# Reordering the loads at the stage boundaries of an eight-core hybrid encoder layer, and dividing the last rows' normalisation between engines

## The chip, the cores and the metric

The program runs on all 8 cores of one Trainium2 chip (two dies, cores 0 to 3 and 4 to 7), one batch entry per core, with no exchange between cores. The metric is device microseconds of the slowest core. An execution can fall into a slow state, in which one die's granted TensorE clock (the share of full speed that the records show for it) is lower: 0.936 on die 1 in the profile of the kernel before. The kernel before takes 3447.7 us (median of 4 executions; the slowest of the four, 3532.0 us, was slow).

## The reference, cut to what matters

One layer of a streaming encoder. One input projection feeds three branches; each is gated, projected to 2048 channels, merged by sigmoid gates, projected once more, added to the input and normalised.

```python
q, k, v, logf, g_fox, b_gate, u, g_conv, mq, g_mem = _project(hp, w_in[l], fox_bf[l])
o_fox = _fox_prompt(q, k, v, logf)                    # 1: forgetting attention, 12 heads
c, tail = _short_conv(u, prev0, conv_w[l], conv_b[l]) # 2: conv, 12 chunks of 128 channels
mk, mv = _mem_kv(mem_prompt, w_mem_kv[l])             #    memory keys/values, between the chunks
o_mem = _mem_attn(mq, mk, mv)                         # 3: memory attention, 20 units
m = g1 * y_fox + g2 * y_conv + g3 * y_mem             # 4: merge stage
h = jnp.einsum('btd,de->bte', m, w_o)                 # 5: output stage, 17 row blocks
return _layernorm(DN_ALPHA * x + h, ln_g, ln_b)
```

Per core there are 2048 prompt rows and 64 sample rows. The kernel runs the five stages in this order.

## The kernel before

A helper records operations in program order for each engine and derives the semaphore waits. Two consequences matter. SP and POOL issue the DMAs, each in its own program order: a DMA whose data is not ready holds up every later DMA of that queue. And a tile placed over an old one waits for all recorded users of the old one.

POOL loads all weights into eight ring slots, when TensorE frees one. SP does nearly everything else: stores, branch tiles `a`, merged tiles `mT`, residual rows `x`, gain `lng` and bias `lnb`.

```python
# conv stage: memory tokens are allocated and loaded only after chunk 1
for c in range(1, 12):
    runall(conv_groups(c, c == 1))
    if c == 1:
        E.settle()
        mem_alloc()            # POOL: memT, mkT, mv
    ...                        # memkv(i): first matmuls on memT follow at once

# memory attention: branch tiles 0 to 3 are loaded in the last of the 20 units
        else:
            for b in range(4):
                load_a(0, b, ABUF[b], d_ab[b])
            E.settle()
...
    load_a(0, 4, ABUF[4], d_ab[4])

# merge stage, last pass (u == 2), last column (j == 15), blocks tb = 0..4
    m, g = ...                                  # ACT: g = sigmoid(bank); DVE: m = bank * g
    mb = g[:, 0:n // 2].bitcast(BF16)           # POOL writes the merged block into g's tile,
    ...                                         # SP stores it: mb_scr[j, :, t0:t0+n] <- mb
    if last and j == 15:
        if tb == 0: mT_load(0, 0); mT_load(1, 0)   # columns 0..14 of 256 merged rows each
        if tb == 1: mT_load(0, 1)                  # column 15
        if tb == 2: mT_load(1, 1)

# output stage
for i in range(2, 9):
    mT_tile(i, XT0 + 8192 * (i - 2))
    mT_load(i, 0)                               # seven loads: six of 1 MB, the last of 0.25 MB
...
load_x32(0)                                     # residual rows, 1 MB, behind all of them
S.add(SP, DMA(lng[:], ...)); S.add(SP, DMA(lnb[:], ...))
load_x32(1)
for tc, (t0, tn) in enumerate(TCH):             # 17 row blocks, 64 matmuls each
    ...                                         # 4 of the 8 PSUM banks per block
    # DVE post: x = alpha * x + bank; bn_stats.  This frees the bank.
    load_x32(tc + 2)
    # ACT normalises, DVE multiplies by lng, POOL adds lnb, SP stores;
    # the last 64 rows in four column pieces through the same three engines
```

`g` has two tiles. So ACT can start on a block only after the mb store of the block before the last has landed.

The softmax here doesn't subtract the row's maximum and nothing guards it: scores larger than these inputs give would overflow.

Of the kernel before, what the change touches and what calls it, by code (L numbers as in the profile page):

```python
# [184 lines left out]
D = 2048  # L185
# [167 lines left out]
def build():  # L353
# [632 lines left out]

    kvq = list(range(16))
    trq = []
    for c in range(1, 12):
        runall(conv_groups(c, c == 1))  # L990
        if c == 1:
            E.settle()
            mem_alloc()
        for g in trq:
            mvtrans(g)
        trq = []
        if c >= 2:
            pass
        n = 2 if c <= 5 else 1
        for _ in range(n):  # L1000
            if kvq:
                i = kvq.pop(0)
                memkv(i)
                if i >= 8 and i % 2 == 1:
                    trq.append((i - 8) // 2)
# [49 lines left out]
    for ui, (h, tb) in enumerate(units):  # L1055
        i = ui % 2
        t0, n = TB[tb]
        parts = [(0, n, 0)] if tb < 4 else [(0, PPART, 0), (PPART, n, 1)]
        pts = []
        for mc in range(2):  # L1060
            sb, rs = BK[3 + mc]
            for (a, b, s) in parts:
                for dc in range(2):
                    E.pe(MM(sb[:, a:b], mem["mkT"][s][:, h * 2 + dc, mc * 128:(mc + 1) * 128], mq[i][0][:, dc, a:b], dc == 0, dc == 1),
                         b - a, [r_mk[s][h * 2 + dc], mq[i][1][dc]], [rs])
            p, rp = mpt.next()
            pts.append((p, rp))
            S.add(ACT, ACTF(p[:, 0:n], sb[:, 0:n], AF.Exp, scale=MSCALE), reads=[rs], writes=[rp])
        if ui + 1 < len(units):
            runall(mproj(units[ui + 1][0], units[ui + 1][1], 1 - i))  # L1070
        else:
            for b in range(4):
                load_a(0, b, ABUF[b], d_ab[b])
            E.settle()
        bl, rbl = BK[7]
        for mc in range(2):
            E.pe(MM(bl[:, 0:n], onesb[:, :], pts[mc][0][:, 0:n], mc == 0, mc == 1), n, [pts[mc][1], r_const], [rbl])
        for dc in range(2):
            ob, ro = BK[5 + dc]
            for (a, b, s) in parts:  # L1080
                for mc in range(2):
                    E.pe(MM(ob[:, a:b], mem["mv"][s][:, mc, h * 2 + dc, :], pts[mc][0][:, a:b], mc == 0, mc == 1),
                         b - a, [r_mv[s][h if s == 0 else mc], pts[mc][1]], [ro])
        l, rrl = mrl.next()
        S.add(ACT, ACTF(l[:, 0:n], bl[:, 0:n], AF.Ln), reads=[rbl], writes=[rrl])
        S.add(ACT, ACTF(l[:, 0:n], l[:, 0:n], AF.Exp, scale=-1.0), reads=[rrl], writes=[rrl])
        def fin(h=h, tb=tb, i=i, n=n, l=l, rrl=rrl):
            for dc in range(2):
                ob, ro = BK[5 + dc]
                o, r = mon.next()  # L1090
                S.add(DVE, TT(o[:, 0:n], ob[:, 0:n], l[:, 0:n], ALU.mult), reads=[ro, rrl], writes=[r])
                a, ra = aom.next()
                S.add(POOL, TT(a[:, 0:n], o[:, 0:n], sgm[i][0][:, dc, 0:n], ALU.mult), reads=[r, sgm[i][1][dc]], writes=[ra])
                S.add(SP, DMA(a_scr[2][tb][:, h * 2 + dc, :], a[:, 0:n]), reads=[ra], writes=[r_as[2][tb]], dmasem=d_ao[id(ra)])
        E.later(1.2, fin)
    E.settle()


    load_a(0, 4, ABUF[4], d_ab[4])
    T0 = Region(SB, ABUF[7] + 10240, SB_HI)  # L1100
    gt = T0.ring("gt", 2, [128, 424], F32)
    mt = T0.ring("mt", 2, [128, 424], F32)
# [30 lines left out]
    def mT_load(i, part):  # L1133
        t, rs, n = mT[i]
        t0 = 256 * i
        j0, j1 = ((0, 15), (15, 16))[part] if i < 2 else (0, 16)
        S.add(SP, DMA(t[:, j0:j1, :], mb_scr[j0:j1, :, t0:t0 + n].rearrange("j p t -> p j t")),
              reads=[r_mb[j][b] for j in range(j0, j1) for b in blks(t0, n)],
              writes=[rs[part]] if i < 2 else rs, dmasem=d_mTs[i])

    for u in range(3):
        last = u == 2
# [10 lines left out]
        for j in range(16):  # L1153
# [8 lines left out]
            for tb in range(5):  # L1162
# [32 lines left out]
                if last and j == 15:  # L1195
                    if tb == 0:
                        mT_load(0, 0)
                        mT_load(1, 0)
                    if tb == 1:
                        mT_load(0, 1)  # L1200
                    if tb == 2:
                        mT_load(1, 1)


    for i in range(2, 9):
        mT_tile(i, XT0 + 8192 * (i - 2))
        mT_load(i, 0)
    L0 = Region(SB, XT0 + 7 * 8192, RG0)
    L1 = Region(SB, ABUF[7] + 10240, TT1)
    X0 = Region(SB, ABUF[2], ABUF[5] + 6784)  # L1210
    NR = 4
    x32 = X0.ring("x32", NR, [128, D], F32)
    d_x32 = {id(r): S.dmasem(f"x32_{i}") for i, (t, r) in enumerate(x32.items)}
    d_yo = {id(r): S.dmasem(f"yo_{i}") for i, (t, r) in enumerate(x32.items)}
    r_ln = [Res("lng"), Res("lnb")]
    lng = L0.tile("lng", [128, D], F32, [r_ln[0]])
    lnb = L1.tile("lnb", [128, D], F32, [r_ln[1]])
    r_stat = [Res(f"stat{i}") for i in range(3)]
    stats = [L0.tile(f"stats{i}", [128, 4, 6], F32, [r_stat[i]]) for i in range(3)]
    mv_ = [L0.tile(f"mv{i}", [128, 4], F32, [r_stat[i]]) for i in range(3)]  # L1220
    xq = {}
    def load_x32(tc):
        if tc >= 17:
            return
        t0, tn = TCH[tc]
        t, r = x32.next()
        xq[tc] = (t, r)
        src = I["xp"][t0:t0 + tn, :] if tc < 16 else I["xs"]
        S.add(SP, DMA(t[0:tn, :], src), writes=[r], dmasem=d_x32[id(r)])
    load_x32(0)  # L1230
    S.add(SP, DMA(lng[:], I["ln_g"].partition_broadcast(128)), writes=[r_ln[0]], dmasem=S.dmasem("lng"))
    S.add(SP, DMA(lnb[:], I["ln_b"].partition_broadcast(128)), writes=[r_ln[1]], dmasem=S.dmasem("lnb"))
    load_x32(1)
    HB = Ring(BK)

    def wo_piece(k):
# [5 lines left out]
    for tc, (t0, tn) in enumerate(TCH):  # L1242
        t, r = xq.pop(tc)
        mt_, rmt, _ = mT[tc // 2]
        o0 = t0 - 256 * (tc // 2)
        hb = [HB.next() for _ in range(4)]
        s = tc % 3
        x = t
        def kmm(db, k):
            w, rw = wo_piece(k)  # L1250
            bk, rb = hb[db]
            E.pe(MM(bk[0:tn, :], mt_[:, k, o0:o0 + tn], w[:, db * 512:(db + 1) * 512], k == 0, k == 15), 512,
                 [rmt[1 if k == 15 else 0], rw], [rb])
        def post(db):
            bk, rb = hb[db]
            c = slice(db * 512, (db + 1) * 512)
            S.add(DVE, STT(x[0:tn, c], x[0:tn, c], DN_ALPHA, bk[0:tn, :], ALU.mult, ALU.add), reads=[rb, r], writes=[r])
            S.add(DVE, lambda e, o_=stats[s][0:tn, db, :], i_=x[0:tn, c]: e.bn_stats(out=o_, in_=i_), reads=[r], writes=[r_stat[s]])
        if tc == 0:
            for k in range(16):  # L1260
                for db in range(4):
                    kmm(db, k)
            for db in range(4):
                post(db)
        else:
            for db in range(4):
                for k in range(16):
                    kmm(db, k)
                post(db)
        load_x32(tc + 2)  # L1270
        m = mv_[s]
        S.add(DVE, lambda e, o_=m[0:tn, 0:2], i_=stats[s][0:tn, :, :].rearrange("p a b -> p (a b)"): e.bn_aggr(out=o_, in_=i_),
              reads=[r_stat[s]], writes=[r_stat[s]])
        S.add(ACT, ACTF(m[0:tn, 2:3], m[0:tn, 1:2], AF.Sqrt, bias=epsb[0:tn, 0:1]), reads=[r_stat[s], r_const], writes=[r_stat[s]])
        S.add(DVE, lambda e, o_=m[0:tn, 2:3]: e.reciprocal(out=o_, in_=o_), reads=[r_stat[s]], writes=[r_stat[s]])
        S.add(DVE, STT(m[0:tn, 3:4], m[0:tn, 0:1], -1.0, m[0:tn, 2:3], ALU.mult, ALU.mult), reads=[r_stat[s]], writes=[r_stat[s]])
        npc = 1 if tc < 16 else 4
        w = D // npc
        rp = [r] if npc == 1 else [Res(f"yp{i}") for i in range(npc)]
        for i in range(npc):  # L1280
            c = slice(i * w, (i + 1) * w)
            S.add(ACT, ACTF(x[0:tn, c], x[0:tn, c], AF.Identity, bias=m[0:tn, 3:4], scale=m[0:tn, 2:3]),
                  reads=[r, r_stat[s]], writes=[rp[i]])
            S.add(DVE, TT(x[0:tn, c], x[0:tn, c], lng[0:tn, c], ALU.mult), reads=[rp[i], r_ln[0]], writes=[rp[i]])
            S.add(POOL, TT(x[0:tn, c], x[0:tn, c], lnb[0:tn, c], ALU.add), reads=[rp[i], r_ln[1]], writes=[rp[i]])
            dst = O["y_p"][t0:t0 + tn, c] if tc < 16 else O["y_s"][:, c]
            S.add(SP, DMA(dst, x[0:tn, c]), reads=[rp[i]], dmasem=d_yo[id(r)])

    import contextlib
    es = contextlib.ExitStack()  # L1290
# [80 lines left out]
```

## Time and profile before

| | |
|---|---|
| fast executions | 3446.3 to 3448.4 us |
| profiled execution | slow: die 0 at clock 0.990, die 1 at 0.936; core 0 (3441.8 us) is read |
| TensorE busy, core 0 | 96% |
| chain that ended last | 90% PE |

The wait list of TensorE on core 0: each line names what PE waited for, the total in us, how often, and the longest. Lines whose longest single wait is under 2 us are left out ("...") where nothing below rests on them.

```profile
PE bank L148 <- DMA memT_134<-memT: 17.4, 1, 17.4
PE bank L148 <- DVE x_147_189 L183: 16.5, 1, 16.5
PE bank L148 <- DMA ring_20_62<-w_in: 13.0, 1, 13.0
PE bank L148 <- DMA ring_23_65<-w_in: 10.6, 1, 10.6
...
PE bank L148 <- DMA a_4_112_154<-a_scr_4: 3.6, 1, 3.6
...
PE bank L148 <- DMA a_0_108_150<-a_scr_0: 2.0, 1, 2.0
...
PE bank L148 <- DMA ring_27_69<-w_o: 0.8, 1, 0.8
```

The two w_in lines are the start of the program. The other lines are stage boundaries: 17.4 us at the first memory matmul, 2.0 + 3.6 us at the merge stage, 16.5 us in the output stage.

PE's timeline at the first and third of these gaps. Columns: start us, duration us, engine, source line, operation, output and inputs, and in brackets the idle time ahead of it.

```profile
1123.62 3.02 PE L148 MATMUL bank<-xT_19_61,ring_27_69 128*128 128x420 bf16 x16
1144.05 3.57 PE L148 MATMUL bank<-memT_134,ring_20_62 128*128 128x256 bf16 x16 [17.42 <-DMA memT_134<-memT]
1147.42 2.10 PE L148 MATMUL bank<-memT_134,ring_21_63 128*128 128x256 bf16 x16
...
3214.20 0.58 PE L148 MATMUL bank<-wob_130_172,mT_139_181 128*128 128x512 bf16 x1 [16.46 <-DVE x_147_189 L183]
3214.58 0.63 PE L148 MATMUL bank<-wob_131_173,mT_139_181 128*128 128x512 bf16 x1
3215.01 0.63 PE L148 MATMUL bank<-wob_132_174,mT_139_181 128*128 128x512 bf16 x1
```

The 16 matmuls behind the first gap take 3.57 us, the next 16 of the same shape 2.10. Behind the other gap matmuls soon start 0.43 us apart (3214.58, 3215.01), for about 5 us, and then 0.216. For some us behind such a gap TensorE thus works at half its rate; it is called cold below. A gap therefore costs more than its wait.

SP's own timeline shows why x is late: it stands in SP's queue behind the mT loads.

```profile
3198.91 3.80 SPq L157 DMA_DIRECT2D mT_146_188<-mb_scr  x1
3202.92 4.00 SPq L157 DMA_DIRECT2D x_147_189<-xp  x1
```

The end of the program, after PE's last matmul ends at 3424.4:

```profile
3427.74 2.93 ACT L165 ACTIVATE x_147_189<-x_147_189,mv_157_199 64x512 f32<-64x512 f32 x4 [0.61 <-DVE mv_157_199 L183]
3428.66 4.72 DVE L175 TENSOR_TENSOR x_147_189<-x_147_189,lng_193 64x512 f32<-64x512 f32 x4 [1.01 <-ACT x_147_189 L165]
3429.48 6.24 POOL L175 TENSOR_TENSOR x_147_189<-x_147_189,lnb_194 64x512 f32<-64x512 f32 x4 [6.85 <-DVE x_147_189 L175]
3431.24 5.02 SPq L157 DMA_DIRECT2D y_s<-x_147_189  x4
```

Four pieces follow each other through three engines; POOL is the slowest, 6.24 us for the four.

### The profile page before, as it was taken

The numbers are of one execution on the slowest core, as the hardware profiler recorded it, in microseconds if no ns is written. First come the engines' busy times: TensorE is split into PE (matmuls) and PEld (weight loads), VectorE is DVE, ScalarE is ACT, GpSimd is POOL, SyncE is SP. The second block draws the span as 40 slices with busy tenths as digits, with TensorE's granted clock in tenths as the row PEclk, the third lists the DMA queues.
The fourth block names the chain that finished last, engine by engine and source line by source line (L and its number), as shares of the span: only waits on it lengthen the run. The fifth ranks groups of instructions, "written<-read, shape, count | busy, mean of one in ns | idle before, by whom it ended". The sixth has DMA issues, their size and how long they took to land.

```text
span 3614.3 us, 54781 instructions; the slowest of 8 cores (3434.6 to 3614.3 us)
## 1 busy us (share of the span) xinstructions
PE 3502.0 (97%) x18761; PEld 1845.2 (51%) x18761; DVE 1202.3 (33%) x2092; ACT 1021.2 (28%) x1846; POOL 771.3 (21%) x962
## 2 busy tenths in 40 slices
PE   6999999999999989999999999999999999999898
PEld 3444444544444545555555554555555555555343
DVE  1455555555556722222222221111111111111365
ACT  1455555555555410010104552111111111111111
POOL 1222222222222211111111221000022223332133
PEclk8888888888888999999999999999999999999999
DMA  9423333333222243333323216333455545655743
GB/s 167 97 64 70 70 70 68 66 67 66 66 63 66 46 69 65 68 62 56 61 50 59 47 38 164 90 98 85 116 143 133 138 118 131 141 125 136 206 173 117
DMA packets 183608, 337.45 MB, mean 93 GB/s; under 512 B 31204, under 2 KB 135388, under 8 KB 177000
## 3 DMA queue, kind: packets, MB, share of 16 engines
q0 software_dynamic: 39744, 134.55, 22.9%
q1 hardware_dynamic: 143592, 199.39, 17.9%
q8 instruction: 156, 2.56, 0.3%
q14 instruction: 116, 0.95, 0.1%
HBM read 362.26 MB, written 106.13 MB: 130 GB/s over the span
## 4 chain that ended last, share of the span: by engine, by line
PE 93%; DMA 3%; SPq 1%; ACT 1%; issue 1%; DVE 1%; POOL 1%; POOLq 0%; DVEq 0%; ACTq 0%
PE bank L148 93%; DMA ring_23_65<-w_in 1%; SPq L157 1%; DMA a_scr_3<-ao_59_101 1%; PE bank L154 0%; DMA memT_134<-memT 0%; DMA mb_scr<-gt_114_156 0%; DMA x_147_189<-xp 0%; DMA a_4_112_154<-a_scr_4 0%; ACT rl_83_125 L165 0%; DVE on_85_127 L175 0%; ACT pt_71_113 L165 0%; POOL ao_59_101 L175 0%; DVE acc_78_120 L175 0%; ACT qT_74 L170 0%
## 5 line engine op out<-in xcount | busy, mean ns | idle before, releaser
L175 DVE TENSOR_TENSOR mt_115_157<-bank,gt_113_155 128x424 f32<-128x424 f32 (+1 forms) x120 | 71.8, 598 | 517.8 <-PE bank L148 448.5
L175 DVE TENSOR_TENSOR mt_116_158<-bank,gt_114_156 128x424 f32<-128x424 f32 (+1 forms) x120 | 71.8, 598 | 494.1 <-PE bank L148 463.9
L165 ACT ACTIVATE gt_113_155<-bank,bm_50 128x424 f32<-128x424 f32 (+1 forms) x120 | 73.6, 613 | 506.3 <-PE bank L148 455.6
L165 ACT ACTIVATE gt_114_156<-bank,bm_50 128x424 f32<-128x424 f32 (+1 forms) x120 | 73.6, 613 | 499.4 <-PE bank L148 470.8
L148 PE MATMUL bank<-xT_15_57,ring_20_62 128*128 128x424 bf16 x400 | 84.5, 359 | 17.9 <-DMA ring_20_62<-w_in 13.9
L148 PE MATMUL bank<-qT_70,kT_71 128*128 128x512 bf16 (+4 forms) x246 | 96.2, 391 | 0.0
L148 PE MATMUL bank<-qT_74,kT_75 128*128 128x512 bf16 (+4 forms) x246 | 94.5, 384 | 0.2 <-DVE st_69_111 L183 0.2
L148 PE MATMUL bank<-xT_17_59,ring_26_68 128*128 128x424 bf16 x416 | 86.2, 352 | 4.8 <-ACT qT_74 L170 4.8
L148 PE MATMUL bank<-xT_17_59,ring_22_64 128*128 128x424 bf16 x416 | 86.8, 354 | 4.0 <-ACT qT_70 L170 4.0
L148 PE MATMUL bank<-xT_16_58,ring_24_66 128*128 128x424 bf16 x432 | 90.2, 353 | 0.0
L148 PE MATMUL bank<-xT_19_61,ring_24_66 128*128 128x420 bf16 x432 | 89.4, 351 | 0.0
L148 PE MATMUL bank<-xT_15_57,ring_24_66 128*128 128x424 bf16 x432 | 89.2, 356 | 0.0
L148 PE MATMUL bank<-xT_17_59,ring_24_66 128*128 128x424 bf16 x432 | 88.7, 353 | 0.0
L148 PE MATMUL bank<-xT_18_60,ring_24_66 128*128 128x420 bf16 x432 | 88.2, 351 | 0.0
L148 PE MATMUL bank<-xT_16_58,ring_26_68 128*128 128x424 bf16 x416 | 87.7, 354 | 0.0
L148 PE MATMUL bank<-xT_16_58,ring_22_64 128*128 128x424 bf16 x416 | 87.2, 354 | 0.0
L148 PE MATMUL bank<-xT_15_57,ring_26_68 128*128 128x424 bf16 x416 | 86.6, 354 | 0.0
L148 PE MATMUL bank<-xT_15_57,ring_22_64 128*128 128x424 bf16 x416 | 86.2, 354 | 0.0
L148 PE MATMUL bank<-xT_19_61,ring_22_64 128*128 128x420 bf16 x416 | 84.9, 351 | 0.3
L148 PE MATMUL bank<-xT_18_60,ring_22_64 128*128 128x420 bf16 x416 | 85.1, 351 | 0.0
L148 PE MATMUL bank<-xT_19_61,ring_26_68 128*128 128x420 bf16 x416 | 84.5, 349 | 0.4 <-ACT qT_74 L170 0.2
L148 PE MATMUL bank<-xT_18_60,ring_26_68 128*128 128x420 bf16 x416 | 84.5, 349 | 0.0
(917 smaller groups left out, 7352.2 us busy)
## 6 DMA issues: line engine op xcount, KB each, us to landing
ring_24_66<-w_in POOLq DMA_DIRECT2D x15, 512.0 KB, 6.7
ring_21_63<-w_in POOLq DMA_DIRECT2D x14, 512.0 KB, 8.0
ring_22_64<-w_in POOLq DMA_DIRECT2D x14, 512.0 KB, 7.8
ring_23_65<-w_in POOLq DMA_DIRECT2D x14, 512.0 KB, 6.8
ring_25_67<-w_in POOLq DMA_DIRECT2D x14, 512.0 KB, 8.2
ring_26_68<-w_in POOLq DMA_DIRECT2D x14, 512.0 KB, 6.7
ring_27_69<-w_in POOLq DMA_DIRECT2D x14, 512.0 KB, 6.6
ring_20_62<-w_in POOLq DMA_DIRECT2D x13, 512.0 KB, 7.1
```

What stands on the lines that cost most here:

```text
L148: return lambda e: e.matmul(out, lhsT=lhsT, rhs=rhs, start=start, stop=stop)
L157: return lambda e: e.dma_start(out=out, in_=in_, **kw)
L165: return lambda e: e.activation(out=out, in_=in_, func=func, **kw)
L175: return lambda e: e.tensor_tensor(out=out, in0=in0, in1=in1, op=op)
```

## The change

The intent is to have every load at its place before the stage that needs it begins, and to shorten the end. Cut to its core:

```diff
+    E.later(16.0, mem_alloc)                 # 16 us into conv chunk 1
     for c in range(1, 12):
         runall(conv_groups(c, c == 1))
-        if c == 1:
-            E.settle()
-            mem_alloc()
...
         else:
-            for b in range(4):
+            E.settle()
+        if ui == 8:                          # unit 8 of 20
+            for b in range(5):
                 load_a(0, b, ABUF[b], d_ab[b])
-            E.settle()
...
-    load_a(0, 4, ABUF[4], d_ab[4])
...
                     if tb == 2:
                         mT_load(1, 1)
-    for i in range(2, 9): ... mT_load(i, 0)
-    load_x32(0)
+                        load_x32(0)
+                    if tb == 3:
+                        load_x32(1)
     # after the last column
     ... lng, lnb ...
-    load_x32(1)
+    mT_load(2, 0)
+    load_x32(2)
+    mT_load(3, 0)
...
-        load_x32(tc + 2)
+        load_x32(tc + 3)
+        if tc % 2 == 0 and tc // 2 + 4 < 9:
+            mT_load(tc // 2 + 4, 0)
...
+        # last 64 rows: columns 1536.. on ACT + POOL, the other three pieces on DVE:
+        #   x = (x - mean) * lng;  x = x * rstd + lnb     (two operations of DVE each)
```

The description that came with the change says that the branch tiles are loaded two units ahead. The code loads them in unit 8 of 20, eleven units ahead of the last.

More of the change, by code (lines that the diff above doesn't have):

```diff
@@ L996, in build @@
         trq = []
-        if c >= 2:
-            pass
         n = 2 if c <= 5 else 1
@@ L1139, in mT_load, with x_alloc, load_x32 @@
               writes=[rs[part]] if i < 2 else rs, dmasem=d_mTs[i])
+    L0 = Region(SB, XT0 + 7 * 8192, RG0)
+    L1 = Region(SB, ABUF[7] + 10240, TT1)
+    X0 = Region(SB, ABUF[2], ABUF[5] + 6784)
+    NR = 4
+    xq = {}
+    x32 = None
+    d_x32, d_yo = {}, {}
+    def x_alloc():
+        nonlocal x32
+        x32 = []
+        for i in range(NR):
+            r = Res(f"x32{i}")
+            d_x32[id(r)] = S.dmasem(f"x32_{i}")
+            d_yo[id(r)] = S.dmasem(f"yo_{i}")
+            x32.append([None, r])
+    def load_x32(tc):
+        if tc >= 17:
+            return
+        t0, tn = TCH[tc]
+        e = x32[tc % NR]
+        if e[0] is None:
+            e[0] = X0.tile(f"x32{tc}", [128, D], F32, [e[1]])
+        t, r = e
+        xq[tc] = (t, r)
+        src = I["xp"][t0:t0 + tn, :] if tc < 16 else I["xs"]
+        S.add(SP, DMA(t[0:tn, :], src), writes=[r], dmasem=d_x32[id(r)])
     for u in range(3):
@@ L1200, in build @@
                         mT_load(0, 1)
+                        x_alloc()
                     if tb == 2:
                         mT_load(1, 1)
-    for i in range(2, 9):
-        mT_tile(i, XT0 + 8192 * (i - 2))
-        mT_load(i, 0)
-    L0 = Region(SB, XT0 + 7 * 8192, RG0)
-    L1 = Region(SB, ABUF[7] + 10240, TT1)
-    X0 = Region(SB, ABUF[2], ABUF[5] + 6784)
-    NR = 4
-    x32 = X0.ring("x32", NR, [128, D], F32)
-    d_x32 = {id(r): S.dmasem(f"x32_{i}") for i, (t, r) in enumerate(x32.items)}
-    d_yo = {id(r): S.dmasem(f"yo_{i}") for i, (t, r) in enumerate(x32.items)}
+                        load_x32(0)
+                    if tb == 3:
+                        load_x32(1)
     r_ln = [Res("lng"), Res("lnb")]
@@ L1220, in build @@
     mv_ = [L0.tile(f"mv{i}", [128, 4], F32, [r_stat[i]]) for i in range(3)]
-    xq = {}
-    def load_x32(tc):
-        if tc >= 17:
-            return
-        t0, tn = TCH[tc]
-        t, r = x32.next()
-        xq[tc] = (t, r)
-        src = I["xp"][t0:t0 + tn, :] if tc < 16 else I["xs"]
-        S.add(SP, DMA(t[0:tn, :], src), writes=[r], dmasem=d_x32[id(r)])
-    load_x32(0)
+    for i in range(2, 9):
+        mT_tile(i, XT0 + 8192 * (i - 2))
     S.add(SP, DMA(lng[:], I["ln_g"].partition_broadcast(128)), writes=[r_ln[0]], dmasem=S.dmasem("lng"))
     S.add(SP, DMA(lnb[:], I["ln_b"].partition_broadcast(128)), writes=[r_ln[1]], dmasem=S.dmasem("lnb"))
-    load_x32(1)
+    mT_load(2, 0)
+    load_x32(2)
+    mT_load(3, 0)
     HB = Ring(BK)
@@ L1276, in build @@
         S.add(DVE, STT(m[0:tn, 3:4], m[0:tn, 0:1], -1.0, m[0:tn, 2:3], ALU.mult, ALU.mult), reads=[r_stat[s]], writes=[r_stat[s]])
-        npc = 1 if tc < 16 else 4
-        w = D // npc
-        rp = [r] if npc == 1 else [Res(f"yp{i}") for i in range(npc)]
-        for i in range(npc):
-            c = slice(i * w, (i + 1) * w)
-            S.add(ACT, ACTF(x[0:tn, c], x[0:tn, c], AF.Identity, bias=m[0:tn, 3:4], scale=m[0:tn, 2:3]),
-                  reads=[r, r_stat[s]], writes=[rp[i]])
-            S.add(DVE, TT(x[0:tn, c], x[0:tn, c], lng[0:tn, c], ALU.mult), reads=[rp[i], r_ln[0]], writes=[rp[i]])
-            S.add(POOL, TT(x[0:tn, c], x[0:tn, c], lnb[0:tn, c], ALU.add), reads=[rp[i], r_ln[1]], writes=[rp[i]])
-            dst = O["y_p"][t0:t0 + tn, c] if tc < 16 else O["y_s"][:, c]
-            S.add(SP, DMA(dst, x[0:tn, c]), reads=[rp[i]], dmasem=d_yo[id(r)])
+        dst = O["y_p"][t0:t0 + tn, :] if tc < 16 else O["y_s"]
@@ new lines, in build @@
+        if tc < 16:
+            S.add(ACT, ACTF(x[0:tn, :], x[0:tn, :], AF.Identity, bias=m[0:tn, 3:4], scale=m[0:tn, 2:3]),
+                  reads=[r, r_stat[s]], writes=[r])
+            S.add(DVE, TT(x[0:tn, :], x[0:tn, :], lng[0:tn, :], ALU.mult), reads=[r, r_ln[0]], writes=[r])
+            S.add(POOL, TT(x[0:tn, :], x[0:tn, :], lnb[0:tn, :], ALU.add), reads=[r, r_ln[1]], writes=[r])
+            S.add(SP, DMA(dst, x[0:tn, :]), reads=[r], dmasem=d_yo[id(r)])
+        else:
+            rp = [Res(f"yp{i}") for i in range(4)]
+            for q in rp:
+                q.w = r.w
+                q.r = dict(r.r)
+            c = slice(1536, 2048)
+            S.add(ACT, ACTF(x[0:tn, c], x[0:tn, c], AF.Identity, bias=m[0:tn, 3:4], scale=m[0:tn, 2:3]),
+                  reads=[rp[3], r_stat[s]], writes=[rp[3]])
+            S.add(POOL, TT(x[0:tn, c], x[0:tn, c], lng[0:tn, c], ALU.mult), reads=[rp[3], r_ln[0]], writes=[rp[3]])
+            S.add(POOL, TT(x[0:tn, c], x[0:tn, c], lnb[0:tn, c], ALU.add), reads=[rp[3], r_ln[1]], writes=[rp[3]])
+            for i in range(3):
+                c = slice(i * 512, (i + 1) * 512)
+                S.add(DVE, STT(x[0:tn, c], x[0:tn, c], m[0:tn, 0:1], lng[0:tn, c], ALU.subtract, ALU.mult),
+                      reads=[rp[i], r_stat[s], r_ln[0]], writes=[rp[i]])
+                S.add(DVE, STT(x[0:tn, c], x[0:tn, c], m[0:tn, 2:3], lnb[0:tn, c], ALU.mult, ALU.add),
+                      reads=[rp[i], r_stat[s], r_ln[1]], writes=[rp[i]])
+                S.add(SP, DMA(dst[:, c], x[0:tn, c]), reads=[rp[i]], dmasem=d_yo[id(r)])
+            S.add(SP, DMA(dst[:, 1536:2048], x[0:tn, 1536:2048]), reads=[rp[3]], dmasem=d_yo[id(r)])
```

## The prediction

> All readings are of core 0 (3441.8 us, granted clock 0.989); die 1 was slow (0.936) in the profiled run, so not used. Reference: the two fast timed runs, 3447 and 3448 us.
>
> **What bounds it.** TensorE: 96% busy on the page, 20.0 of 20 us at clock 1.00 in nearly every stretch after 1150 us (windows view), 90% of the chain of waits. Such a change can win only stage-boundary gaps. PE's waits, longest first: memory tokens 17.4 us, residual row 0 (DVE on x, behind its DMA) 16.5, w_in at the start 13.0 and 10.6, branch tiles a_4 3.6 and a_0 2.0.
>
> **Terms (timeline):**
> 1. Memory tokens. Issued at 1130.1, after the settle behind conv chunk 1, landing 13.8 us later; PE stands from 1126.6 to 1144.05. The change issues them 16 us into that chunk (about 1085), where the DMA share is near zero. Wait 17.4 -> 0. PE then runs cold: 16 matmuls take 3.57 us, the next 16 take 2.10. Gain 17.4 + 1.5 = 18.9.
> 2. Branch tiles. Four loads together near the end of the memory stage land after 12.7 to 25 us, the fifth later. Waits 2.0 + 3.6; the groups behind them took 3.99 and 4.36 instead of 2.31, the next 3.63 instead of 3.03. Gain 10. The loads move to memory unit 8. There 6.4 MB hold up the SP queue for an estimated 28 us (rate of the old loads), so an attention store behind them delays POOL and DVE. Rings of 3 and 2 tiles and units of 12.7 us should absorb it; I allow 0 to 3 us.
> 3. Residual rows. Row tile 0 is issued at 3202.9 behind seven mT loads and lands at 3213.3; only then can DVE free the PSUM banks that row 2 needs. Wait 16.5, then about 13 matmuls at 0.427 instead of 0.216 us, 2.7. Issued at about 3170 it lands before row 0 ends (3183.8). Gain 19. POOL's last w_o weight (9.6 us to land, 0.8 us wait) now competes with row tiles: perhaps 1 to 2 us lost.
> 4. Tail. From PE's end (3424.4) to the last y_s issue (3435.9) are 11.5 us, four pieces serially through ACT, DVE and POOL (6.24 us). Now three pieces take two DVE operations each (about 0.7 us) and the fourth ACT plus two on POOL (about 1.5 each), in parallel. Estimate: 2.5 us less.
>
> Sum 50.4, less 1.4 for contention: 49 us. The Trainium skill, "TensorE: Matmul & The Clock Gate", section "What's actually happening", says the default state is throttled and activity releases it; this trace agrees (0.427 -> 0.216 us after the 16.5 us gap).
>
> **Predicted:** 3399 us, 8 in 10 between 3388 and 3417: 1.4% faster. Faster by over 2%: 0.03; within 2%: 0.96; slower by over 2%: 0.01.
>
> **Signs.** PE's wait list has no memT, a_0, a_4 or x over 1 us; memory DMA shows at 1085 to 1110; the three boundaries show clock 1.00; rows run 13.8 us each without a break; the tail after PE is about 15 us instead of 17.4. Failing steps would show as a wait on ring w_o at k = 14, 15 of row 0, on mT, on lng before row 3, or on attention banks around units 10 to 12.
>
> **What would make it wrong.** Row loads ahead of mb stores delaying ACT and the banks; early branch loads stalling attention; denser work lowering the granted clock.

## The result, and the profile after

The changed kernel takes 3406.2 us (median of 4; fast ones 3405.5 to 3406.4) against 3447.7: 41.6 us less (41.1 between the medians of the fast executions). The ratio is 0.988, 95% interval 0.9858 to 0.9903. A ratio is the mean time of one kernel's fast executions over that of the other's from the same rounds, so it is not quite the ratio of the medians. The profiled execution is fast, cores 3395.3 to 3403.9 us.

The wait list of core 0 after, the same view as before:

```profile
PE bank L148 <- DMA ring_20_62<-w_in: 12.7, 1, 12.7
PE bank L148 <- DMA ring_23_65<-w_in: 10.6, 1, 10.6
...
PE bank L148 <- DMA mT_138_180<-mb_scr: 5.2, 1, 5.2
...
PE bank L148 <- DMA ring_27_69<-w_o: 3.4, 1, 3.4
...
PE bank L148 <- DMA ring_26_68<-w_o: 1.4, 1, 1.4
```

memT, a_0, a_4 and x are gone. In their place there are three waits in the output stage: 5.2 us on the first merged tile and 4.8 us (3.4 + 1.4) on the last two w_o weights. PE's timeline shows the mended boundaries and then the new gaps:

```profile
1123.05 3.02 PE L148 MATMUL bank<-xT_19_61,ring_27_69 128*128 128x420 bf16 x16
1125.91 1.91 PE L148 MATMUL bank<-memT_134,ring_20_62 128*128 128x256 bf16 x16
...
1993.11 3.03 PE L148 MATMUL bank<-xT_15_57,ring_20_62 128*128 128x424 bf16 x16
1995.98 2.31 PE L148 MATMUL bank<-a_0_108_150,ring_21_63 128*128 128x424 bf16 x12
...
3136.53 1.59 PE L148 MATMUL bank<-a_4_129_171,ring_27_69 128*128 128x420 bf16 x8
3143.31 1.87 PE L148 MATMUL bank<-wob_130_172,mT_138_180 128*128 128x512 bf16 x4 [5.18 <-DMA mT_138_180<-mb_scr]
...
3158.98 1.02 PE L148 MATMUL bank<-ring_26_68,mT_138_180 128*128 128x512 bf16 x4 [1.42 <-DMA ring_26_68<-w_o]
3163.37 1.86 PE L148 MATMUL bank<-ring_27_69,mT_138_180 128*128 128x512 bf16 x4 [3.37 <-DMA ring_27_69<-w_o]
```

The lines with x4 also show the cold clock again: 1.87 and 1.86 us behind the 5.2 and 3.4 us gaps, 1.02 otherwise.

SP's timeline for the last merge column says where the first gap comes from:

```profile
3131.12 1.91 SPq L157 DMA_DIRECT2D mT_139_181<-mb_scr  x1
3133.08 5.52 SPq L157 DMA_DIRECT2D pv_119_161<-m_scr_3  x1
3138.71 0.37 SPq L157 DMA_DIRECT2D mb_scr<-gt_113_155  x1
3139.12 0.43 SPq L157 DMA_DIRECT2D mT_138_180<-mb_scr  x1
...
3144.82 0.33 SPq L157 DMA_DIRECT2D x_140_182<-xp  x1
3145.72 0.32 SPq L157 DMA_DIRECT2D mb_scr<-gt_113_155  x1
3146.19 1.34 SPq L157 DMA_DIRECT2D x_141_183<-xp  x1
```

Behind mT(0) and mT(1), nearly 1 MB each, SP spends 5.52 us issuing a 210 KB load; the mb store behind it (of block 1) leaves only at 3138.71, after the last merge matmul (end 3138.12). Column 15 of mT(0), which row 0 needs, stands right behind that store: it leaves at 3139.12 and takes 3.8 us to land. That is the first gap on this core. ACT, too, must wait for that store before it may overwrite the gate tile, as its timeline shows:

```profile
3142.85 0.61 ACT L165 ACTIVATE gt_113_155<-bank,bm_50 128x420 f32<-128x420 f32 x1 [11.73 <-DMA mb_scr<-gt_113_155]
```

Behind ACT wait DVE, POOL's merged blocks, and, because POOL issues in order, the last two w_o weights (on cores 2 and 4 it is this late ACT, not mT(0), that ends PE's first wait). POOL's timeline:

```profile
3145.59 1.07 POOL L175 TENSOR_TENSOR gt_114_156<-mt_116_158,pv_117_159 128x420 bf16<-128x420 f32 x1
3146.60 0.57 POOL L157 DMA_DIRECT2D ring_26_68<-w_o  x1
```

Then the weights share the DMA engines with x(0), x(1) and lng. The list of DMA issues (operation, count, KB, us from issue to landing):

```profile
ring_26_68<-w_o POOLq DMA_DIRECT2D x1, 512.0 KB, 12.2
ring_27_69<-w_o POOLq DMA_DIRECT2D x1, 512.0 KB, 16.1
```

The same list of the kernel before:

```profile
ring_26_68<-w_o POOLq DMA_DIRECT2D x1, 512.0 KB, 6.6
ring_27_69<-w_o POOLq DMA_DIRECT2D x1, 512.0 KB, 9.6
```

To see what each stage gained, the rest uses a table made from PE's timeline, all 8 cores averaged: "conv gap" is from the end of conv chunk 1 to the first matmul of chunk 2 (it holds two memory groups, 3.3 us when nothing waits); "merge" is from its first to the end of its last matmul; "output" from there to PE's end; "tail" from PE's end to the end of the span. Conv and memory attention between them take 863.7 to 864.5 us in every run.

| us, mean of cores | conv gap | merge | output | tail | span |
|---|---|---|---|---|---|
| before, fast profile (run base) | 22.5 | 1154.2 | 256.0 | 17.4 | 3439.5 |
| after | 3.3 | 1145.0 | 246.7 | 16.2 | 3400.4 |
| gained | 19.2 | 9.2 | 9.3 | 1.2 | 39.1 |

Each row comes from one execution. How far another one may lie off can be read from a_taildve (below), which is the changed kernel but for the last rows: its output stage is 245.8 us, and the wait at the start of row 0 has a mean of 2.3 us against 3.4.

### The profile page after: what moved, and what is told of

Read it like the earlier page. It is cut to its first block, busy times and chain, and to the rows that moved or that the text cites. A ratio compares the mean times of both kernels' runs of the same rounds, so it can differ in the third digit from the quotient of the medians.

```text
span 3403.9 us, 54778 instructions; the slowest of 8 cores (3395.3 to 3403.9 us)
## 1 busy us (share of the span) xinstructions
PE 3320.0 (98%) x18761; PEld 1788.5 (53%) x18761; DVE 1223.0 (36%) x2094; ACT 1012.8 (30%) x1843; POOL 770.6 (23%) x960
## 4 chain that ended last, share of the span: by engine, by line
PE 94%; DMA 2%; ACT 1%; DVE 1%; POOL 1%; issue 1%; SPq 0%; ACTq 0%; DVEq 0%; POOLq 0%
PE bank L148 94%; DMA ring_23_65<-w_in 1%; DMA ring_27_69<-w_o 0%; PE bank L154 0%; SPq L157 0%; DVE st_69_111 L183 0%; POOL hl_82_124 L175 0%; DVE on_85_127 L175 0%; DVE x_140_182 L183 0%; ACT rl_84_126 L165 0%; ACT qT_74 L170 0%; POOL hl_80_122 L175 0%; ACT qT_70 L170 0%; ACT pt_73_115 L165 0%; POOL hl_81_123 L171 0%
## 5 line engine op out<-in xcount | busy, mean ns | idle before, releaser
L148 PE MATMUL bank<-xT_15_57,ring_20_62 128*128 128x424 bf16 x400 | 81.6, 351 | 16.7 <-DMA ring_20_62<-w_in 12.7
L148 PE MATMUL bank<-xT_17_59,ring_26_68 128*128 128x424 bf16 x416 | 82.7, 342 | 6.0 <-ACT qT_74 L170 6.0
L148 PE MATMUL bank<-xT_17_59,ring_22_64 128*128 128x424 bf16 x416 | 82.8, 342 | 5.0 <-ACT qT_70 L170 5.0
L148 PE MATMUL bank<-xT_16_58,ring_24_66 128*128 128x424 bf16 x432 | 86.1, 342 | 0.0
L148 PE MATMUL bank<-xT_19_61,ring_24_66 128*128 128x420 bf16 x432 | 85.4, 340 | 0.0
L148 PE MATMUL bank<-xT_17_59,ring_24_66 128*128 128x424 bf16 x432 | 84.7, 342 | 0.0
L148 PE MATMUL bank<-qT_74,kT_75 128*128 128x512 bf16 (+4 forms) x246 | 84.4, 343 | 0.2 <-DVE st_69_111 L183 0.2
L148 PE MATMUL bank<-qT_70,kT_71 128*128 128x512 bf16 (+4 forms) x246 | 84.5, 343 | 0.0
L148 PE MATMUL bank<-xT_15_57,ring_24_66 128*128 128x424 bf16 x432 | 84.4, 342 | 0.0
L148 PE MATMUL bank<-xT_18_60,ring_24_66 128*128 128x420 bf16 x432 | 84.4, 340 | 0.0
L148 PE MATMUL bank<-xT_16_58,ring_26_68 128*128 128x424 bf16 x416 | 83.7, 342 | 0.0
L148 PE MATMUL bank<-xT_16_58,ring_22_64 128*128 128x424 bf16 x416 | 83.2, 342 | 0.0
L148 PE MATMUL bank<-xT_15_57,ring_22_64 128*128 128x424 bf16 x416 | 82.6, 343 | 0.0
L148 PE MATMUL bank<-xT_15_57,ring_26_68 128*128 128x424 bf16 x416 | 82.5, 342 | 0.0
L148 PE MATMUL bank<-xT_19_61,ring_26_68 128*128 128x420 bf16 x416 | 81.4, 340 | 0.9 <-ACT qT_74 L170 0.3
L148 PE MATMUL bank<-xT_19_61,ring_22_64 128*128 128x420 bf16 x416 | 81.2, 340 | 0.7
L148 PE MATMUL bank<-xT_18_60,ring_26_68 128*128 128x420 bf16 x416 | 81.4, 340 | 0.0
L148 PE MATMUL bank<-xT_18_60,ring_22_64 128*128 128x420 bf16 x416 | 81.4, 340 | 0.0
```

Of the source, the lines that this page charges most:

```text
L148: return lambda e: e.matmul(out, lhsT=lhsT, rhs=rhs, start=start, stop=stop)
```

## The experiments

Each was run for three rounds beside the kernel before on the same chip, but for one look at a_taildve. There were three chips: base and the first three p_ runs; the a_ runs; the rest. A median given for a run counts its slow executions too (two of five in p_mem, one of four in p_rows, a_mt1, a_xsplit, p_xfirst and best2); the median of the fast ones is lower by at most 1.3 us.

### base: the kernel before again

No edit.

> The kernel before, unchanged, to get a profile in the fast state: the first one was slow on die 1, so the two dies were out of step while core 0 was read. Theory A (the backlog at the end of the merge stage belongs to the old kernel too once both dies run in step): cores end near 3444 to 3446 us, and core 0 shows a PE wait of 3 to 6 us at the start of output row 0 (on mT or on ACT's gate tile) beside the 16 us wait on x. Theory B (the change made the backlog): that wait stays at or under 2 us, cores end near 3442. Timed ratio 1.000 either way.

Measured: 3445.8 us, ratio 1.0001. The profile is fast, cores 3433.6 to 3445.1 us. The wait at the start of output row 0 is 1.0 us on core 0 and 0 to 3.3 us on the others, mean 1.5. Theory A expected 3 to 6 us and falls for core 0; two cores (3.1 and 3.3 us) do show it. The old kernel had a small part of the backlog already. This profile is the baseline of all tables.

### p_mem, p_branch, p_rows: one part of the change alone

Edits: the first hunk of the diff; the second and third; the output-stage hunks with the old tail.

> Only the memory-token load moved into conv chunk 1. Predicted term 18.9 us: 3429 us, ratio 0.9945. Rival (part of the gain is lost later because the next weights are late): under 15 us.

> Only the branch loads moved to memory unit 8. Predicted term 10 us: 3437.5 us, ratio 0.9971. Rival (the blocked attention store costs PE time around units 10 to 12): under 7 us.

> Only the reordering of residual rows, mT and layer-norm loads, old tail. Predicted term 19 us less 1 to 2: 3430 us, ratio 0.995. Rival, from comparing core 0 of the two traces (36.6 us gained at PE's end against 30.2 at the end of the merge stage): the term is only 6 to 10 us, because PE now waits 3 to 5 us at the start of row 0 and 3 to 5 us on the last two w_o weights: 3438 to 3441 us, ratio 0.997 to 0.998.

| run | median us | ratio (95%) | conv gap | merge | output | tail |
|---|---|---|---|---|---|---|
| p_mem | 3429.0 | 0.995 (0.9931 to 0.997) | 3.3 | 1154.5 | 256.4 | 17.7 |
| p_branch | 3436.4 | 0.9974 (0.9957 to 0.9992) | 22.2 | 1145.0 | 255.7 | 17.4 |
| p_rows | 3436.9 | 0.9973 (0.9954 to 0.9993) | 22.0 | 1154.2 | 245.1 | 17.4 |

Memory tokens and branch tiles give what was predicted, in their own stage, and nothing is lost elsewhere. In the changed kernel an attention store behind the early branch loads took 25.3 us to land and POOL waited 12.3 us for it, yet PE had no wait there. The rows part gives 10.9 us in its stage instead of 19 less 1 to 2: the rival was nearer. The wait on x is gone (16.6 us mean), but a wait of 5.1 us on the last w_o weights has come.

### a_mt1: the second merged tile is loaded later

```diff
                     if tb == 0:
                         mT_load(0, 0)
-                        mT_load(1, 0)
...
                     if tb == 2:
-                        mT_load(1, 1)
                         load_x32(0)
                     if tb == 3:
+                        mT_load(1, 0)
+                        mT_load(1, 1)
                         load_x32(1)
```

> After, with both loads of the second mT tile moved from the first and third block of the last merge column to just before row tile 1; that tile is first needed 28 us into the output stage. Theory A (the 1 MB of mT(1) in front of the mb stores of the last column makes them late, so row 0 starts late): PE's wait at the start of row 0 (mean over cores 3.4 us) falls to 1 us or less, POOL issues the last two w_o weights about 5 us earlier and their wait also falls below 2 us; the output stage from the end of the last merge matmul to PE's end goes from 246.7 to 238 to 241 us. Rival B (general memory traffic makes the stores late, not this load): the stage stays within 2 us of 246.7, or the wait moves to row 2 on mT(1).

Measured: 3398.8 us (fast 3396.1 to 3400.1), ratio 0.9859, interval 0.984 to 0.9878. The output stage is 236.2 us. The start-of-row wait falls from 3.4 to 0.5 us and the wait on w_o from 4.7 to 0.5 us; the weights are issued 3.1 us earlier (5 expected), and the stage falls further than expected. SP's timeline on core 0, to be held against the one of the changed kernel:

```profile
3130.24 1.80 SPq L157 DMA_DIRECT2D pv<-m_scr  x1
3132.14 0.37 SPq L157 DMA_DIRECT2D mb_scr<-gt  x1
```

The small load is issued in 1.80 instead of 5.52 us, and the mb store leaves 6.6 us earlier (3138.71 to 3132.14, in programs whose merge stages ended 1.0 us apart). Theory A holds: with one early load of 1 MB out of the way, first needed 28 us later, the wait is nearly gone. The load is not the whole cause: in base this load stood at the same place, and the wait was 1.5 us.

### a_xlate: only row tile 0 stays ahead

```diff
-                    if tb == 3:
-                        load_x32(1)
...
+    mT_load(2, 0)
     ... lng, lnb ...
-    mT_load(2, 0)
+    load_x32(1)
```

> After, with row tile 1, gain and bias moved behind mT(2); only row tile 0 (1 MB) stays ahead. Theory C (the 3 MB of row and layer-norm loads share the DMA engines with the last two w_o weights): the PE wait on those weights falls from about 4.5 us per core to 1.5 us or less and the output stage to about 242 us. Rival D (POOL issues those weights late, because ACT waits for the mb store): wait stays at 3 us or more. The wait at the start of row 0 (3.4 us) stays in both.

Measured: five of the six executions were slow; the fast one took 3399.9 us. In the profile die 0 was slow; cores 4 to 7 were undisturbed and are used: output 242.6 us, start-of-row wait 4.1 us, wait on w_o 1.6 us. Theory C's 242 us is met and its 1.5 us nearly; the start-of-row wait stays, as expected. D falls: the weights were issued no earlier (7.4 us after the merge stage against 6.5), but landed in 10.3 us instead of 13.7.

### a_xsplit: shorter runs, same bytes

```diff
+        if tc < 2:
+            for i in range(4):
+                c = slice(i * 512, (i + 1) * 512)
+                S.add(SP, DMA(t[0:tn, c], src[:, c]), writes=[r], dmasem=d_x32[id(r)])
...
```

> After, with row tiles 0 and 1 loaded in four column pieces each: same bytes at the same place in the queue, runs of 2 KB instead of 8 KB. Theory E ([...]longer runs of the row tiles take a larger share from the w_o weights): wait on w_o falls below 2.5 us per core. Theory F (bytes count, not run length): it stays at 4 to 5 us and the stage at 246 to 248 us.

Measured: 3405.9 us, ratio 0.9881 (0.9861 to 0.99); output 246.6 us; wait on w_o 4.2 us. Theory E falls between 8 KB and 2 KB.

### p_membranch: two parts, without the rows

> Memory tokens and branch tiles together, rows and tail as before. Additive: 17.5 + 10 us less than before, about 3419 us, ratio 0.992. Theory I (with both gaps gone all cores reach the output stage at the same moment, and their mT loads then compete, which is why the wait at the start of row 0 is 3.4 us in the changed kernel but 1.2 us with the rows change alone): that wait, mean over cores, rises here to 2.5 us or more. Rival J (it comes from the reordered rows): it stays at 1.2 to 1.6 us as before.

Measured: 3419.7 us, ratio 0.9921 (0.9907 to 0.9936): additive, but for an output stage of 257.9 us against 256.0. The start-of-row wait rises to 3.0 us, although the rows are as before; J falls, as far as one profile of each can tell. Either part alone leaves the wait at 1.6 us (p_mem) and 1.7 (p_branch), so it seems to take both. That all cores then arrive at the same moment is consistent with I (conv gap and merge are 3.3 and 1145.0 us on every core, against 21.7 to 23.5 and 1151.1 to 1156.6 before), but the records have no common clock for the cores, so it is argued and not shown.

### p_xfirst: one move in the kernel before

```diff
-    for i in range(2, 9):
-        mT_tile(i, XT0 + 8192 * (i - 2))
-        mT_load(i, 0)
...
     load_x32(1)
+    for i in range(2, 9):
+        mT_tile(i, XT0 + 8192 * (i - 2))
+        mT_load(i, 0)
```

> The kernel before with one move only: the loads of mT(2) to mT(8) stand after the row, gain and bias loads instead of ahead of them; nothing is put ahead of the mb stores. Theory K (the 16.6 us wait is only the row tile's place in the SP queue): the wait on x goes below 1 us and the output stage from 256.0 to 237 to 241 us, so this one move beats the row part of the change (245.1 us): 3428 to 3432 us, ratio 0.995 to 0.9965. Rival L: row loads beside the last w_o weights cost as much here as in the row part: stage 244 us or more.

Measured: 3434.6 us, ratio 0.9963 (0.9946 to 0.998); output 242.5 us; no wait on x, 4.1 us on w_o. The wait on x was only its place in SP's queue, so K's cause is right. Its size is not: 242.5 lies between K's 241 and L's 244. The row and gain loads beside the last weights cost 4 us even when they are ahead of no mb store.

### How late the last two w_o weights are

Mean over cores, us: when POOL issues the first of them after the end of the merge stage, how long the two take to land on average, and PE's waits.

| run | issue | landing | wait on w_o | wait at start of row 0 |
|---|---|---|---|---|
| base | 4.9 | 7.7 | 0.1 | 1.5 |
| p_rows | 4.9 | 12.9 | 5.1 | 1.2 |
| p_xfirst | 4.7 | 10.9 | 4.1 | 1.4 |
| after | 6.5 | 13.7 | 4.7 | 3.4 |
| a_xsplit | 6.6 | 12.2 | 4.2 | 3.3 |
| a_xlate (cores 4 to 7) | 7.4 | 10.3 | 1.6 | 4.1 |
| a_mt1 | 3.4 | 7.7 | 0.5 | 0.5 |
| best2 (below) | 3.0 | 9.5 | 2.8 | 0.3 |

Two things add up: late issue (the mb store) and slow landing (what else is in flight). In the old kernel the sum, 12.6 us, was just enough, since row 0 needs these weights last. A third thing decides what is enough: how soon row 0 gets to them. By PE's timeline, less the wait on w_o, it would have got there 14.0 us after the merge stage in base, but 9.6 us in best2, where it starts earlier. So nearly the same sum (12.5) costs best2 2.8 us. The Trainium skill, "DMA: Bandwidth & Descriptors", section "Issuing engines are not separate DMA queues", says that DMAs started by different engines run on the same 16 DMA engines and interleave. This agrees: a load of POOL's queue took 7.7 or 13.7 us by what SP had issued.

### a_taildve: the last rows on DVE alone

```diff
-            ... c = slice(1536, 2048) on ACT, POOL, POOL
-            for i in range(3):
+            for i in range(4):
```

> After, with all four pieces of the last rows on DVE, POOL and ACT unused there. Theory G (DVE operations with two SBUF operands slow down while POOL runs its tensor operations on SBUF): all eight DVE operations take 0.74 us, none 1.5 us or more, and the tail from PE's end to the end of the span stays about 16.2 us although DVE has a third more to do. Rival H (the long DVE operations come from something else, such as the stores): the long ones remain, tail 18 us or more.

Measured: the fast one of two executions took 3404.6 us. The tail is 15.2 us on every core, against 16.2 for the changed kernel. DVE's middle operations in the changed kernel, while POOL worked from 3392.12 to 3395.57:

```profile
3392.04 0.74 DVE L183 SCALAR_TENSOR_TENSOR x_140_182<-x_140_182,mv_148_190,lnb_185 64x512 f32<-64x512 f32 x1 [0.18 <-DVE x_140_182 L183]
3392.71 1.74 DVE L183 SCALAR_TENSOR_TENSOR x_140_182<-x_140_182,mv_148_190,lng_184 64x512 f32<-64x512 f32 x1
3394.56 1.56 DVE L183 SCALAR_TENSOR_TENSOR x_140_182<-x_140_182,mv_148_190,lnb_185 64x512 f32<-64x512 f32 x1
3396.05 0.73 DVE L183 SCALAR_TENSOR_TENSOR x_140_182<-x_140_182,mv_148_190,lng_184 64x512 f32<-64x512 f32 x1
```

The same position with POOL idle:

```profile
3392.83 0.74 DVE L183 SCALAR_TENSOR_TENSOR x<-x,mv,lng 64x512 f32<-64x512 f32 x1
3393.67 0.74 DVE L183 SCALAR_TENSOR_TENSOR x<-x,mv,lnb 64x512 f32<-64x512 f32 x1
```

All eight take 0.73 or 0.74 us: G holds, and the tail even shortened. The Trainium skill, "SBUF — State Buffer", section "SBUF: two separate sides", says that DVE operations with two SBUF inputs and GpSimd operations that read SBUF take turns on one port pair, held for a whole instruction. The trace agrees: 1.74 and 1.56 us beside POOL, 0.74 alone.

### best and best2: faster than both kernels

`best` is a_mt1 with a_taildve's tail. `best2` puts nothing but mT(0) ahead of the last mb stores:

```diff
+    load_x32(0)
+    mT_load(1, 0)
+    mT_load(1, 1)
     ... lng ...
+    load_x32(1)
     ... lnb ...
     mT_load(2, 0)
```

(The same loads are taken out of the last merge column.)

> After, with mT(1) loaded late (as in a_mt1) and the last rows on DVE alone (as in a_taildve). The two gains add: output stage 236 us, tail 15.2 us, about 3396 to 3397 us, ratio 0.9855.

> As best, but nothing besides mT(0) ahead of the last mb stores: row tile 0, mT(1), gain, row tile 1, bias after the last merge column, in this order. Theory A and C: waits at the start of row 0 and on w_o at most 0.5 us mean, output stage 235 us, 3395 us. Rival: gain or row tile 1 now late, PE waits at row 2 or 3 on DVE's x: stage 238 us or more.

Measured: best 3394.1 us (four fast executions, 3391.9 to 3395.9), ratio 0.9847 (0.9833 to 0.9862), output 237.0 us, tail 15.2 us. The gains add, and the version beats the changed kernel by about 12 us (medians; no run had the two side by side). Their fast executions do not overlap (3391.9 to 3395.9 and 3405.5 to 3406.4), but the intervals of the two ratios just touch. best2 takes 3399.2 us, ratio 0.9861 (0.9842 to 0.9881), output 239.7 us. Neither of its two expectations was right: no wait on x came, but w_o still costs 2.8 us. The rival's stage of 238 us or more is met, for another reason. The weights took 9.5 us to land in best2 and 7.7 in best. mT(1) was in flight beside them in both (issued 5.6 and 4.8 us after the merge stage, mean of the cores), and gain and row tile 1 came later in both (15.9 and 16.3 us in best2, 13.5 and 10.8 in best). What differs is row tile 0: in best it was issued 3.7 us before the end of the merge stage and had landed 4.0 us after it, when the weights were just being issued (3.5); in best2 it was issued 4.1 us after the end and landed at 16.1, together with the last weight (16.0). Row tile 0 ahead of the last mb stores did less harm than row tile 0 beside the weights.

## Why the prediction was right, and where it was not

The total was right: 3399 us, range 3388 to 3417, measured 3406.2; within 2% as stated. The range was wide enough to take in one term that gave half of what was forecast. Its terms:

1. **Memory tokens: right.** 18.9 us predicted, 19.2 in the stage. The cold clock behind the gap belongs to it: the first memory group takes 1.91 instead of 3.57 us now.
2. **Branch tiles: right.** 10 us predicted, 9.2 measured. The rings absorbed the blocked store; the allowance of 0 to 3 us was not needed.
3. **Residual rows: cause right, size wrong.** The wait on x is gone and its cause is shown (p_xfirst). But "Gain 19 ... perhaps 1 to 2 us lost" was 9.3 us in the changed kernel. The mis-sized term is what the reordered loads do to others. The wait on w_o went from 0.1 to 4.7 us, the wait at the start of row 0 from 1.5 to 3.4, and matmuls run cold behind both. The rise of the second comes with the other two parts, not with the rows (3.0 us in p_membranch, 1.2 in p_rows). The prediction listed the very wait that came among its failing signs, "a wait on ring w_o at k = 14, 15 of row 0", and "row loads ahead of mb stores" as the danger; it set 1 to 2 us for what cost about 5. It did not see that mT(1), which the change left where it was, already stood ahead of one of them, and that taking it away (a_mt1) returns 10.5 us of the stage.
4. **Tail: half.** 2.5 us predicted, 1.2 measured. The step that failed was "in parallel": DVE and POOL did not run at their own speeds side by side.

The clock did not fall: 0.994 to 0.995 in the fast profile after, 0.989 to 0.991 before, because fewer gaps make PE cold: core 0's clock records show half speed for 75.3 us of the span in base and 41.5 after. The Trainium skill's description of the clock gate ("TensorE: Matmul & The Clock Gate", "What's actually happening") was a good guide to this: PE's rate halved behind each gap of 3.4 us and more that is shown here, and came back after a few us.

Part of the 41.6 us against 39.1 is that the slowest core is timed, while the table averages cores; the slowest cores of the two profiles are 41.2 us apart.

## What to carry to other kernels

Moving a load earlier on an in-order queue also moves it ahead of other work: for each moved transfer, list what stands behind it, what shares the engines with it while it flies, and who waits for those. When the longest wait of a boundary is taken away, the next one is often only a few us shorter (here weights that used to land just in time), so time the second-latest arrival before you count the gain. Splitting a short tail over engines that share SBUF access may be slower than one engine alone (a tail of 16.2 us against 15.2 here).

## What the Trainium skill lacked or had wrong

- "TensorE: Matmul & The Clock Gate", section "Seeing it yourself", says to budget a clock of 13/16 (0.81) once three cores of a die run dense matmuls. In fast executions of the changed kernel all eight cores ran at a mean granted clock of 0.993 to 0.996, with PE 98% busy (core 0 of the profile), and no core of any fast profile had 13/16 for more than 15.1 us. The level itself does show: in the two slow profiles the four cores of the slow die stood at 13/16 for 723 to 1087 us (before, die 1; a_xlate, die 0) and otherwise nearly always at 1. The clocks of 0.82 to 0.97 that slow executions list for a die are thus, in these two, means of 13/16 and 1. What starts and ends it is not shown. An execution of 9.1 ms with clock 1.0 on all cores, and one of 14.3 ms in which two cores took 9.1 ms at clock 1.0 and the others had 0.23 to 0.68, stay unexplained.
- "DMA: Bandwidth & Descriptors" says that queues interleave, but gives no figure for how much one load slows beside another queue: here 512 KB weight loads took 7.7 us beside mT loads (base) and 12.9 us beside row and gain loads (p_rows); runs of 2 KB instead of 8 KB changed that by 1.5 us at most. Why mT (512-byte runs) disturbs less stays open.
- "SBUF — State Buffer" has the shared port pair right, but no duration for the case here: a DVE operation of 64 x 512 fp32 with two SBUF inputs took 1.56 to 1.74 us beside POOL, 0.74 alone.
- No page read here says how long SP itself is held when much is queued: 5.52 us to issue one 210 KB load behind 1.9 MB of mT loads, 0.4 us for the like of it when little is queued.
